# A second, narrower form for pairs of experts that hold few tokens

## The chip, the cores and the metric

The kernel runs on one core of one Trainium2 chip (trn2). The metric is device time in microseconds (us) of one execution. Three runs of the kernel before gave 617.62, 618.52 and 620.73 us; the median is 618.52 us.

## What is computed

One layer of a diffusion backbone over 256 tokens of width 1024, all in float32: modulation, a normalisation, three branches (a convolution, a neighbourhood attention, a recurrence), and then a mixture of 16 experts, which is what the change touches:

```python
    out = jnp.zeros_like(h)
    for e in range(N_EXPERTS):
        he = jax.nn.silu(h @ w1[e]) * (h @ w3[e])
        out = out + gate[..., e:e + 1] * (he @ w2[e])
    return out
```

`h` is 256 x 1024, `w1` and `w3` are 1024 x 512 and `w2` is 512 x 1024 for each expert. `gate` is zero but for the two experts that the router picks for a token, so an expert has to work on its own tokens alone. How many these are depends on the data. With the inputs that the reference draws, the fuller expert of the pairs 0 to 7 (experts 0 and 1, 2 and 3, and so on) holds 55, 42, 15, 14, 49, 72, 29 and 41 tokens.

## The kernel before

The whole program is one function, `tile_kernel`. Its first 370 us compute the branches and are not touched. After the router, the experts are done in eight pairs, `p` = 0 to 7, one after the other. TensorE (PE) executes its instructions in the order in which the code is written; the other engines are ordered by the scheduler of the recording layer.

**The weights.** A pair has 24 tiles of 128 x 1024 floats (512 KB): eight of `w1`, eight of `w3` (`i` = 0, 1) and eight of `w2` (`i` = 2). All 192 are read in the order of `ew_order` (L102): the pairs in turn, and in a pair `w1`, `w3`, `w2`. On chip there is room for 35 of them (`SPAN`, L111) and two more that are placed at the start. `freed(n)` (L1347) tells that n tiles are done with, and `load_experts` (L117) issues the next n loads, the first 31 from GpSimd's queue (POOL), the others from SyncE's (SP). A load waits for the instructions that last read the tile whose place it takes; eight loads at most are under way, since each waits for the one eight before it.

**One pair.** An expert gets 64 columns for its tokens. `open_group` (L1337) gathers the tokens of two pairs (PE product with a one-hot matrix, ACT writes `xg`). `pair_slots` (L1343) transposes the one-hot matrix (`oT`) and gathers the gates (`gsl`). `product` (L1153) multiplies: for each eighth `k` of the 1024 inputs one matmul for each expert `s` of the pair, the expert's 64 token columns as weights in one half of the array, 512 columns of `w1` or `w3` streamed. The two experts' matmuls stand in different halves of the array's columns. `silu` (L1166), `weigh` (L1169), `hidden` (L1173: transposes, and ACT copies to `heT`), `rows` (L1180: the products with `w2`, q = 0, 1 for the two halves of the output, f = 0 to 3 for its four tiles), `split_rows` (L1186: ACT and DVE write the result `ys` in two parts) and `scatter` (L1190: PE puts the rows back to their tokens with `oT`, DVE adds to the output `xl`) end the pair.

**More than 64 tokens.** `extra` (L1204) does 32 further tokens of each expert, in four column groups: the two experts by two halves of the width (`phe`, `pye`). It stands in conditionals on the number of tokens, which every engine reads into a register (`count`, L1308); `further` (L1315) nests them up to 256 tokens. In `second` (L1326) this ladder is one branch of a conditional, and `w3`'s product without extra tokens the other. `expect` (L1311) writes a hint for PE ahead of the branch.

**The order of PE.** In the loop of L1366, pair p's `w3` product is followed by the next group's gather (after odd p), the next pair's slots, `hidden`, `rows`, then two steps of the next pair's `w1` product (`ahead`), the scatter of pair p, and the rest of the next `w1` product. So PE has matmuls of the next pair while ACT and DVE split this pair's rows. Of the 24 tiles of a pair p > 1, `freed(16)` stands behind `second`, and `freed(8)` behind the rows; for p < 2 three times 8.

**Pair 7** has its own form: halves of 256 columns, `last_rows` and `finish` by quarters of the output, and the output's DMAs.

Of the kernel before, what the change touches and what calls it, by code (L numbers as in the profile page):

```python
# [10 lines left out]
F32R = mybir.dt.float32r  # L11
# [39 lines left out]
def tile_kernel(ctx, tc, x_all, cc, vecs, mod_a, mod_b, w_k, w_rx, w_v, w_in, rnn_w, rpb_t, w_br, w_out,  # L51
# [9 lines left out]
    def mm_bank(shape=(128, 512), name="mm"):  # L61
        return psum.tile(list(shape), F32, tag="mm", name=name, bufs=4)
# [1090 lines left out]
    def product(p, i, ph, h=None):  # L1153

        xg, xo = group[p // 2][0], p % 2 * 128
        cols = slice(0, 512) if h is None else slice(256 * h, 256 * h + 256)
        for k in range(KD):
            for s in range(2):
                c = xo + 64 * s
                w, at = quarter(p, i, s, k, h or 0)  # L1160
                at = at if h is not None else slice(at.start, at.start + 512)
                pe.matmul(ph[64 * s:64 * s + 64, cols], xg(k)[:, c:c + 64], w[:, at], start=k == 0 and not h,  # L1162
                          stop=k == KD - 1, skip_group_check=True)
            yield

    def silu(ph, c=slice(0, 512)):  # L1166
        act.activation(sl[:, c], ph[:, c], AF.Silu)  # L1167

# [11 lines left out]
    def rows(p, py, f, q):  # L1180

        for s in range(2):
            pe.matmul(py[q][64 * s:64 * s + 64, :], heT[f // 2][:, f % 2, 64 * s:64 * s + 64],  # L1183
                      ew[p][2][f][s][:, q * 512:q * 512 + 512], start=f == 0, stop=f == 3, skip_group_check=True)

    def split_rows(py, q):  # L1186
        c = slice(q * 512, q * 512 + 512)
# [112 lines left out]
    def run(steps):  # L1300
        for _ in steps:
            pass
# [7 lines left out]

    def expect(p):  # L1311

        tc.mark_branch_hint_location(f"more{p}", hint=counts[p] > 64, engines=(mybir.EngineType.PE,))

    def further(p, n):  # L1315

# [5 lines left out]
    def more(p):  # L1322

        further(p, 64)

    def second(p, ph0, ph):  # L1326

        with tc.If(counts[p] > 64, label=f"more{p}") as c:
            extra(p, 64, product(p, 1, ph))
            further(p, 96)  # L1330
            silu(ph0)
        with c.Else():
            silu(ph0)
            for _ in product(p, 1, ph):
                pass
# [7 lines left out]
    def pair_slots(p):  # L1343
        c = p % 2 * 128
        return slots(p, [x[:, c:c + 128] for x in group[p // 2][1]], 64)

    def freed(n):  # L1347
        room[0] += n
        load_experts()
# [13 lines left out]
            more(0)  # L1363
    oT, gsl = pair_slots(0)
    run(w1)
    for p in range(7):  # L1366
        ph = mm_bank(name="ph1")
        if p > 1:
            second(p, ph0, ph)
            freed(16)  # L1370
        else:

            if p:
                more(p)
            freed(8 if p else 8 - len(brief))
            silu(ph0)
            run(product(p, 1, ph))
            freed(8)
        for q in range(2):
            weigh(gsl, ph, q)  # L1380
        if p % 2:
            run(open_group(p // 2 + 1))
        oT_ = oT
        oT, gsl = pair_slots(p + 1)
        ph0 = mm_bank(name="ph0")
        w1 = product(p + 1, 0, ph0, 0 if p == 6 else None)
        for q in range(2):
            hidden(q)
        py = [ax_bank(name="py0"), ax_bank(name="py1")]
        for q in range(2):  # L1390
            for f in range(4):
                rows(p, py, f, q)
            split_rows(py, q)
        freed(8)

        ahead(w1, 2)
        scatter(lambda i, m: ys[i][:, m * 128:m * 128 + 128], lambda m: oT_)
        count(p + 1)
        ahead(w1, 1)
        expect(p + 1)  # L1400
        run(w1)


    more(7)
# [150 lines left out]
```

## Time and profile before

| what | us |
|---|---|
| median of three runs | 618.52 |
| the profiled execution, its own time | 616.12 |
| its span, first to last instruction | 614.3 |
| outside the span | 1.8 |
| PE busy | 580.2 (94%) |
| DVE, ACT, POOL busy | 349.1, 259.8, 19.4 |
| DMA over the span | 170.65 MB, mean 278 GB/s |

The granted TensorE clock is 0.999 of 2.4 GHz over the span. The page cuts the span in 40 slices: in the last third, where the experts are, PE's digit is 8 or 9 until the last slice and the DMA queues move 400 GB/s and more, but for a slice with 226 GB/s near 540 us. Busy time of PE counts matmuls that overlap in the array once; "x" counts records, and a float32 matmul leaves two of them. A branch is not counted as busy on any engine.

### The profile page before, as it was taken

The numbers are of one execution on the slowest core, as the hardware profiler recorded it, in microseconds if no ns is written. First come the engines' busy times: TensorE is split into PE (matmuls) and PEld (weight loads), VectorE is DVE, ScalarE is ACT, GpSimd is POOL, SyncE is SP. The second block draws the span as 40 slices with busy tenths as digits, with TensorE's granted clock in tenths as the row PEclk, the third lists the DMA queues.
The fourth block names the chain that finished last, engine by engine and source line by source line (L and its number), as shares of the span: only waits on it lengthen the run. The fifth ranks groups of instructions, "written<-read, shape, count | busy, mean of one in ns | idle before, by whom it ended". The sixth has DMA issues, their size and how long they took to land. (4 is left out here: it accounts for less than half of the span.)

```text
span 614.3 us, 10619 instructions
## 1 busy us (share of the span) xinstructions
PE 580.2 (94%) x4127; PEld 408.1 (66%) x4127; DVE 349.1 (57%) x797; ACT 259.8 (42%) x456; POOL 19.4 (3%) x42
## 2 busy tenths in 40 slices
PE   1899999999999899999999988999999999999986
PEld 0789888778788778888899975335445334454454
DVE  4667899999758968988469554121240314132303
ACT  4345446654598765877545624203012111130101
POOL 0000000000000000103112010000000000000000
PEclk9999999999999999999999999999999999999999
DMA  8983874446853463759969776999999999969961
GB/s 256 367 339 114 310 259 154 137 141 193 278 212 103 138 241 103 236 176 356 313 211 379 283 245 226 388 360 406 402 393 407 407 408 409 398 226 409 409 248 68
DMA packets 51825, 170.65 MB, mean 278 GB/s; under 512 B 5664, under 2 KB 10016, under 8 KB 51744
## 3 DMA queue, kind: packets, MB, share of 16 engines
q1 hardware_dynamic: 46704, 151.26, 67.2%
q0 software_dynamic: 5040, 18.35, 8.6%
q8 instruction: 46, 0.75, 0.5%
q14 instruction: 35, 0.29, 0.1%
HBM read 168.54 MB, written 1.05 MB: 276 GB/s over the span
## 5 line engine op out<-in xcount | busy, mean ns | idle before, releaser
L1162 PE MATMUL ph<-ew,xg 128*64 128x512 f32 (+1 forms) x576 | 115.6, 548 | 3.5 <-PEq L1318 2.8
L73 ACT ACTIVATE w<-raw 128x1024 fp32r<-128x1024 f32 x68 | 71.8, 1056 | 65.6 <-PE gps L69 11.6
L74 DVE TENSOR_TENSOR w<-raw,w 128x1024 fp32r<-128x1024 f32 x68 | 82.9, 1219 | 21.5 <-ACT w L73 20.8
L1162 PEld LDWEIGHTS ph<-ew,xg 128*64 128x64 f32 x576 | 41.5, 137 | 66.0 <-issue 58.3
L70 PE MATMUL gps<-h,w 128*128 128x256 f32 x192 | 55.2, 288 | 1.2 <-DVE w L74 1.2
L68 PE MATMUL gps<-h,w 128*128 128x256 f32 x192 | 56.0, 291 | 0.4 <-DVE y L934 0.4
L69 PE MATMUL gps<-h,w 128*128 128x256 f32 x192 | 54.5, 284 | 0.0
L593 DVE SCALAR_TENSOR_TENSOR cacc<-up,vc,cacc 128x243 f32<-128x243 f32 (+14 forms) x120 | 52.1, 472 | 1.4 <-ACT cacc L585 0.7
L1171 DVE SCALAR_TENSOR_TENSOR he<-sl,gsl,ph 128x256 f32<-128x256 f32 x16 | 7.1, 477 | 77.5 <-PE ph L1162 76.2
L1183 PE MATMUL py<-ew,heT 128*64 128x512 f32 x224 | 49.6, 595 | 1.2 <-ACT heT L1178 0.8
L74 DVE TENSOR_TENSOR ys<-py,ys 128x512 fp32r<-128x512 f32 (+1 forms) x18 | 11.4, 633 | 58.0 <-ACT ys L73 58.0
L68 PEld LDWEIGHTS gps<-h,w 128*128 128x128 f32 x192 | 36.6, 191 | 4.2 <-issue 2.6
L70 PEld LDWEIGHTS gps<-h,w 128*128 128x128 f32 x192 | 36.7, 191 | 2.8 <-issue 1.5
L69 PEld LDWEIGHTS gps<-h,w 128*128 128x128 f32 x192 | 36.7, 191 | 0.9 <-issue 0.7
L1183 PEld LDWEIGHTS py<-ew,heT 128*64 128x64 f32 x224 | 15.5, 137 | 30.8 <-issue 26.0
L1201 DVE SCALAR_TENSOR_TENSOR xl<-scp,g,xl 128x256 f32<-128x256 f32 x72 | 29.2, 475 | 7.5 <-PE scp L1197 7.5
L1167 ACT ACTIVATE sl<-ph 128x512 f32<-128x512 f32 (+1 forms) x9 | 5.0, 550 | 63.1 <-PE ph L1162 40.4
L73 ACT ACTIVATE ys<-py 128x512 fp32r<-128x512 f32 (+1 forms) x18 | 9.9, 550 | 50.5 <-PE py L1183 36.6
L114 POOL DMA_DIRECT2D ew<-in_w_exp x31 | 16.6, 537 | 321.1 <-ACT pp L813 248.8
L1119 ACT ACTIVATE xg<-gps,b2m 128x256 f32<-128x256 f32 x32 | 13.4, 471 | 22.7 <-PE gps L1115 21.8
L349 PE MATMUL mps<-ma,cs 128*32 128x256 f32 (+1 forms) x160 | 10.1, 397 | 13.2 <-DMA ma<-in_mod_a 13.1
L1197 PEld LDWEIGHTS scp<-oT,ys 128*128 128x128 f32 x128 | 15.7, 188 | 6.7 <-issue 5.2
(358 smaller groups left out, 1310.0 us busy)
## 6 DMA issues: line engine op xcount, KB each, us to landing
ew<-in_w_exp SPq DMA_DIRECT2D x161, 512.0 KB, 10.2
raw<-in_w_in SPq DMA_DIRECT2D x40, 512.0 KB, 4.4
ew<-in_w_exp POOLq DMA_DIRECT2D x31, 512.0 KB, 7.3
raw<-in_mod_b SPq DMA_DIRECT2D x28, 512.0 KB, 4.1
ma<-in_mod_a SPq DMA_DIRECT2D x12, 512.0 KB, 10.0
raw<-in_w_br SPq DMA_DIRECT2D x12, 512.0 KB, 4.0
raw<-in_w_out SPq DMA_DIRECT2D x8, 512.0 KB, 7.5
ma<-in_mod_a SPq DMA_DIRECT2D x8, 256.0 KB, 6.7
```

The source lines that it names most:

```text
L68: pe.matmul(ps, wh, xh, start=start, stop=False, skip_group_check=True)
L69: pe.matmul(ps, wh, xl_, start=False, stop=False, skip_group_check=True)
L70: return pe.matmul(ps, wl, xh, start=False, stop=stop, skip_group_check=True)
L73: act.activation(hi, src, AF.Copy)
L74: dve.tensor_tensor(lo, src, r32(hi), op=ALU.subtract)
L114: queue.dma_start(t, w_exp[6 * p + 2 * i + s, :, 1024 * q:1024 * q + 1024])
L593: dve.scalar_tensor_tensor(cacc[:, b, i0:i1], up[:, b, i0 + o:i1 + o], half_d[:, b * 31 + j:b * 31 + j + 1], cacc[:, b, i0:i1], op0=ALU.mu ...
L1119: act.activation(place(k0 + j), ps[:, j, :], AF.Identity, bias=b2m[:, k0 + j:k0 + j + 1])
L1162: pe.matmul(ph[64 * s:64 * s + 64, cols], xg(k)[:, c:c + 64], w[:, at], start=k == 0 and not h, stop=k == KD - 1, skip_group_check=True)
L1183: pe.matmul(py[q][64 * s:64 * s + 64, :], heT[f // 2][:, f % 2, 64 * s:64 * s + 64], ew[p][2][f][s][:, q * 512:q * 512 + 512], start=f == ...
L1197: pe.matmul(ps[:, j, :], rows_(i, m), toks(m), start=(j == 0 and i == 0), stop=i == parts - 1, skip_group_check=True)
L1201: dve.scalar_tensor_tensor(xl[:, m, :], ps[:, j, :], g2[:, m:m + 1], xl[:, m, :], op0=ALU.mult, op1=ALU.add)
```

## The change

Pair 0 stays, pair 7 stays, and pairs 1 to 6 get two conditionals in a row: more than 32 tokens takes `wide_pair`, fewer than 33 takes `narrow_pair`. `wide_pair` has the products of before. `narrow_pair` gives each expert 32 columns and splits the width over two column groups, so that four matmuls (two experts by two halves) stand in the array side by side; it moves a copy of `oT` and `gsl` up by 32 partitions with POOL (`oTb`), so that the scatter finds the second half of the output in the other column group.

What crosses from one pair to the next moves with it: the `w1` product of the next pair no longer starts behind the rows, the previous pair's scatter stands in front of the conditional (eight blocks of the output for odd p, four for even p, whose other four stand inside), and the 24 tiles are freed together behind both conditionals. The `py` banks come from the other pool.

```diff
+    def product_small(p, i, ph):
+        xg, xo = group[p // 2][0], p % 2 * 128
+        for k in range(KD):
+            for s in range(2):
+                for h in range(2):
+                    w, at = quarter(p, i, s, k, h)
+                    c = 64 * s + 32 * h
+                    pe.matmul(ph[c:c + 32, :256], xg(k)[:, xo + 64 * s:xo + 64 * s + 32], w[:, at], start=k == 0,
+                              stop=k == KD - 1, skip_group_check=True)
...
+    def rows_small(p, py):
+        for f in range(4):
+            for s in range(2):
+                for q in range(2):
+                    c, x = 64 * s + 32 * q, 64 * s + 32 * (f // 2)
+                    pe.matmul(py[c:c + 32, :], heT[0][:, f % 2, x:x + 32], ew[p][2][f][s][:, q * 512:q * 512 + 512],
+                              start=f == 0, stop=f == 3, skip_group_check=True)
...
-    for p in range(7):
-        ph = mm_bank(name="ph1")
-        if p > 1:
-            second(p, ph0, ph)
-            freed(16)
-        else:
-            if p:
-                more(p)
-            freed(8 if p else 8 - len(brief))
-            silu(ph0)
-            run(product(p, 1, ph))
-            freed(8)
+    def wide_pair(p, oT, oTb, gsl, toks, ms):
+        ph0, ph = mm_bank(name="ph0"), mm_bank(name="ph1")
+        pool.tensor_copy(oTb, oT)
+        w1 = product(p, 0, ph0)
+        ahead(w1, 1)
+        expect(p)
+        run(w1)
+        second(p, ph0, ph)
+        guess(f"narrow{p}", counts[p] < 33)
         for q in range(2):
             weigh(gsl, ph, q)
-        if p % 2:
-            run(open_group(p // 2 + 1))
-        oT_ = oT
-        oT, gsl = pair_slots(p + 1)
-        ph0 = mm_bank(name="ph0")
-        w1 = product(p + 1, 0, ph0, 0 if p == 6 else None)
+        scatter_rows(toks, ms)
         for q in range(2):
             hidden(q)
-        py = [ax_bank(name="py0"), ax_bank(name="py1")]
+        py = [mm_bank(name="py0"), mm_bank(name="py1")]
         for q in range(2):
             for f in range(4):
                 rows(p, py, f, q)
             split_rows(py, q)
-        freed(8)
-        ahead(w1, 2)
-        scatter(lambda i, m: ys[i][:, m * 128:m * 128 + 128], lambda m: oT_)
+    def narrow_pair(p, oT, oTb, gsl, toks, ms):
+        ph0, ph = mm_bank(name="ph0"), mm_bank(name="ph1")
+        product_small(p, 0, ph0)
+        pool.memset(r32(oTb), 0.0)
+        for s in range(2):
+            a, b = slice(64 * s, 64 * s + 32), slice(64 * s + 32, 64 * s + 64)
+            pool.tensor_copy(oTb[b], oT[a])
+            pool.tensor_copy(gsl[b], gsl[a])
+        silu(ph0, slice(0, 256))
+        product_small(p, 1, ph)
+        weigh(gsl, ph, 0)
+        scatter_rows(toks, ms[:2])
+        hidden(0)
+        scatter_rows(toks, ms[2:])
+        py = mm_bank(name="py0")
+        rows_small(p, py)
+        for q in range(2):
+            split_rows([py, py], q)
...
+    for p in range(1, 7):
+        guess(f"wide{p}", counts[p] > 32)
+        if p % 2 == 0:
+            run(open_group(p // 2))
+        if p > 1:
+            oT, gsl = pair_slots(p)
+        oTb = work.tile([128, T], F32R, name="oTb", bufs=2)
+        n = 8 if p % 2 else 4
+        scatter_rows(toks, range(n))
+        with tc.If(counts[p] > 32, label=f"wide{p}"):
+            wide_pair(p, oT, oTb, gsl, toks, range(n, 8))
+        with tc.If(counts[p] < 33, label=f"narrow{p}"):
+            narrow_pair(p, oT, oTb, gsl, toks, range(n, 8))
+        freed(24)
+        toks = oT, oTb
         count(p + 1)
-        ahead(w1, 1)
-        expect(p + 1)
-        run(w1)
+    expect(7)
+    oT, gsl = pair_slots(7)
+    ph0 = mm_bank(name="ph0")
+    w1 = product(7, 0, ph0, 0)
+    ahead(w1, 2)
+    scatter_rows(toks, range(8))
+    run(w1)
```

`guess` is the hint of `expect` with a label of the caller's. Pair 0 stands in front of the loop, written out: `w3`'s product, `count(1)` and the slots of pair 1, `hidden`, `rows`, with `freed` of 6, 8 and 8 tiles as before.

The order of SyncE's loads, first in the program before, from the load that takes the first place left by pair 1's `w1` onward (`ew` with a number is one weight tile, and the names in brackets are the engines whose counters the load waits for: PE, or the earlier loads DMAHW and DMASW):

```order
L114 DMA ew_6579<-in_w_exp 128x1024 [waits DMAHW4_49,DMASW0_49,PE_49]
L114 DMA ew_6581<-in_w_exp 128x1024 [waits DMAHW5_49,DMASW1_49,PE_49]
L114 DMA ew_6600<-in_w_exp 128x1024 [waits DMAHW6_49,DMASW2_49,PE_49]
L114 DMA ew_6602<-in_w_exp 128x1024 [waits DMAHW7_49,PE_49]
L114 DMA ew_6604<-in_w_exp 128x1024 [waits DMAHW0_49,PE_49]
L114 DMA ew_6606<-in_w_exp 128x1024 [waits DMAHW1_49,PE_49]
```

And in the changed program, the last three loads into places of pair 0 and the first four into places of pair 1:

```order
L114 DMA ew_5540<-in_w_exp 128x1024 [waits DMAHW3_49,DMASW7_49,PE_49]
L114 DMA ew_5542<-in_w_exp 128x1024 [waits DMAHW4_49,DMASW0_49,PE_49]
L114 DMA ew_5544<-in_w_exp 128x1024 [waits DMAHW5_49,DMASW1_49,PE_49]
L114 DMA ew_6741<-in_w_exp 128x1024 [waits DMAHW6_49,PE_49]
L114 DMA ew_6743<-in_w_exp 128x1024 [waits DMAHW7_49]
L114 DMA ew_6745<-in_w_exp 128x1024 [waits DMAHW0_49]
L114 DMA ew_6747<-in_w_exp 128x1024 [waits DMAHW1_49]
```

Before, each load waits for PE at its own place in the pair; now the first of the 24 waits, and the count it waits for is reached in the second half of the narrow form's rows (or when that form has been skipped), so it stands for the whole pair, and those behind it wait only for earlier loads.

The order of PE behind the rows of pair 0, in the program before (`py` the rows, `ph` the `w1` product of pair 1, `scp` the scatter):

```order
L1183 MATMUL py_5496<-ew,heT 64x512 x8
L1162 MATMUL ph_5486<-ew,xg 64x512 x4
L1197 MATMUL scp<-oT,ys 128x256 x16
L1309 TENSOR_LOAD cnt
L1162 MATMUL ph_5486<-ew,xg 64x512 x2
L1313 REGISTER_ALU
L1541 BRANCH_PREFETCH_HINT
L1162 MATMUL ph_5486<-ew,xg 64x512 x10
```

and in the changed program, from the rows of pair 0 to the start of pair 1's `w1` product:

```order
L1195 MATMUL py_5509<-ew,heT 64x512 x8
L1337 REGISTER_ALU
L1618 BRANCH_PREFETCH_HINT
L1218 MATMUL scp<-oT,ys 128x256 x16
L1465 COMPARE_AND_BRANCH
L1162 MATMUL ph_5579<-ew,xg 64x512 x2
```

The four matmuls of the next pair that stood between the rows and their scatter are behind the branch now.

PE in pair 2 of the changed program, from the end of the wide form to the end of the narrow one:

```order
L1195 MATMUL py_7939<-ew,heT 64x512 x8
L1465 UNCONDITIONAL_BRANCH x2
L1467 COMPARE_AND_BRANCH
L1175 MATMUL ph_7961<-ew,xg 32x256 x32
L1175 MATMUL ph_7962<-ew,xg 32x256 x32
L1218 MATMUL scp<-oTb,ys 128x256 x4
L1189 MATMUL hp<-ident,he 128x128 x2
L1218 MATMUL scp<-oTb,ys 128x256 x4
L1204 MATMUL py_8052<-ew,heT 32x512 x16
```

The narrow form stands behind the whole wide form with its ladder of `extra`, so a narrow pair jumps over that, and a wide pair jumps over the narrow form.

## Rows read from the trace of the kernel before

**Rows 1.** The page, part 1, and its DMA issues from POOL.
```profile
PE 580.2 (94%) x4127; PEld 408.1 (66%) x4127; DVE 349.1 (57%) x797; ACT 259.8 (42%) x456; POOL 19.4 (3%) x42
...
ew<-in_w_exp POOLq DMA_DIRECT2D x31, 512.0 KB, 7.3
```

**Rows 2.** Windows: length, PE, PEld, DVE, ACT, POOL busy, clock, DMA share, GB/s.
```profile
404.00:410.00 6.00, 5.96 (x30) 2.08 (x28) 2.50 (x7) 0.00 (x0) 0.00 (x0) 1.00 1.03 409
...
460.00:500.00 40.00, 39.58 (x210) 17.37 (x207) 6.90 (x18) 6.57 (x15) 0.00 (x0) 1.00 1.03 407
...
536.00:547.00 11.00, 10.15 (x75) 7.18 (x72) 4.79 (x11) 4.24 (x10) 0.00 (x0) 1.00 0.51 163
```

**Rows 3.** PE's timeline, end of pair 2 to pair 3's rows: start, length, last waits.
```profile
448.33 7.09 PE L1183 MATMUL py<-ew,heT 128*64 128x512 f32 x32
455.24 1.89 PE L1162 MATMUL ph<-ew,xg 128*64 128x512 f32 x8
457.06 2.15 PE L1197 MATMUL scp<-oT,ys 128*128 128x256 f32 x16
459.14 12.24 PE L1162 MATMUL ph<-ew,xg 128*64 128x512 f32 x56
471.31 4.07 PE L1115 MATMUL gps<-oh,hT 128*128 128x256 f32 x32
475.21 0.38 PE L1141 MATMUL ohp<-ident,oh 128*128 128x128 f32 x2
475.43 0.51 PE L1146 MATMUL pg<-gate,oh 128*128 128x2 f32 x4
```

**Rows 4.** The chain of waits that ended last: start, length.
```profile
587.91 7.13 PE ph L1162 x64
...
606.72 1.90 PE py L1419 x16
```

**Rows 5.** SyncE's weight loads, issued 350 to 410 us, 410 to 441, 535 to 600.
```profile
L114 SPq DMA_DIRECT2D ew<-in_w_exp x28: 327/373/940, 358.2 to 403.0; - x28
...
L114 SPq DMA_DIRECT2D ew<-in_w_exp x25: 327/328/1090, 410.1 to 440.7; - x25
...
L114 SPq DMA_DIRECT2D ew<-in_w_exp x37: 327/328/924, 542.0 to 584.3; - x37
...
DMA to landing us min/median/max: 5.4/10.2/11.9
```

**Rows 6.** PE's timeline, the extra tokens of pair 5: `phe` and `pye` in four column groups.
```profile
517.59 2.13 PE L1220 MATMUL gpe<-hT,ohe 128*128 128x512 f32 x8
...
522.17 7.11 PE L1241 MATMUL phe<-ew,heT 128*32 128x256 f32 x128
...
532.46 3.64 PE L1258 MATMUL pye<-ew,heT 128*32 128x512 f32 x32
...
542.40 4.03 PE L1115 MATMUL gps<-oh,hT 128*128 128x256 f32 x32 [0.85 <-PEq L1318]
```

**Rows 7.** PE's timeline, pairs 0, 4 and 7.
```profile
393.76 7.09 PE L1183 MATMUL py<-ew,heT 128*64 128x512 f32 x32
...
508.39 1.89 PE L1162 MATMUL ph<-ew,xg 128*64 128x512 f32 x8
...
587.91 7.13 PE L1162 MATMUL ph<-ew,xg 128*64 128x256 f32 x64 [2.61 <-PEq L1318]
...
606.65 1.95 PE L1419 MATMUL py<-ew,heT 128*64 128x256 f32 x16
```

**Rows 8.** Groups by form, 380 to 614 us, DVE and ACT: mean ns.
```profile
L74 DVE TENSOR_TENSOR ys<-py,ys 128x512 fp32r<-128x512 f32 x14 | 9.7, 692 | 51.3 <-ACT ys L73 51.3
L1171 DVE SCALAR_TENSOR_TENSOR he<-sl,gsl,ph 128x256 f32<-128x256 f32 x16 | 7.1, 477 | 77.5 <-PE ph L1162 76.2 <-ACT sl L1167 1.3
...
L73 ACT ACTIVATE ys<-py 128x512 fp32r<-128x512 f32 x14 | 8.4, 597 | 43.7 <-PE py L1183 36.6 <-issue 7.1
L1178 ACT ACTIVATE heT<-hp 128x256 f32<-128x256 f32 x16 | 5.9, 388 | 6.2 <-PE hp L1177 6.0
```

**Rows 9.** Branch instructions by source line, PE's: duration ns min/median/max.
```profile
L1318 PEldq COMPARE_BRANCH  x4: 3341/3572/4750, 375.9 to 583.0; - x4
...
L1328 PEldq COMPARE_BRANCH  x6: 89/3688/4074, 435.4 to 559.6; - x6
```

**Rows 10.** The branch of pair 2's `second` on PE.
```profile
L1328 PEldq COMPARE_BRANCH  x1: 3524/3524/3524, 435.4 to 435.4; - x1
```

More of the change, by code (lines that the diff above doesn't have):

```diff
@@ L1311, in expect, with guess @@
     def expect(p):
-        tc.mark_branch_hint_location(f"more{p}", hint=counts[p] > 64, engines=(mybir.EngineType.PE,))
+        guess(f"more{p}", counts[p] > 64)
+    def guess(label, cond):
+        tc.mark_branch_hint_location(label, hint=cond, engines=(mybir.EngineType.PE,))
     def further(p, n):
@@ L1365, in tile_kernel, with scatter_rows @@
     run(w1)
-    for p in range(7):
-        ph = mm_bank(name="ph1")
-        if p > 1:
-            second(p, ph0, ph)
-            freed(16)
-        else:
-            if p:
-                more(p)
-            freed(8 if p else 8 - len(brief))
-            silu(ph0)
-            run(product(p, 1, ph))
-            freed(8)
+    def scatter_rows(toks, ms):
+        scatter(lambda i, m: ys[i][:, m * 128:m * 128 + 128], lambda m: toks[m // 4], ms)
+    def wide_pair(p, oT, oTb, gsl, toks, ms):
[7 more added lines that the diff above has]
+        guess(f"narrow{p}", counts[p] < 33)
         for q in range(2):
             weigh(gsl, ph, q)
-        if p % 2:
-            run(open_group(p // 2 + 1))
-        oT_ = oT
-        oT, gsl = pair_slots(p + 1)
-        ph0 = mm_bank(name="ph0")
-        w1 = product(p + 1, 0, ph0, 0 if p == 6 else None)
+        scatter_rows(toks, ms)
         for q in range(2):
             hidden(q)
-        py = [ax_bank(name="py0"), ax_bank(name="py1")]
+        py = [mm_bank(name="py0"), mm_bank(name="py1")]
         for q in range(2):
@@ L1393, in tile_kernel @@
             split_rows(py, q)
-        freed(8)
-        ahead(w1, 2)
-        scatter(lambda i, m: ys[i][:, m * 128:m * 128 + 128], lambda m: oT_)
-        count(p + 1)
-        ahead(w1, 1)
-        expect(p + 1)
-        run(w1)
+    def narrow_pair(p, oT, oTb, gsl, toks, ms):
[16 more added lines that the diff above has]
+            split_rows([py, py], q)
+    ph = mm_bank(name="ph1")
+    freed(8 - len(brief))
+    silu(ph0)
+    run(product(0, 1, ph))
+    freed(8)
+    for q in range(2):
+        weigh(gsl, ph, q)
+    count(1)
+    toks = oT, oT
+    oT, gsl = pair_slots(1)
+    for q in range(2):
+        hidden(q)
+    py = [mm_bank(name="py0"), mm_bank(name="py1")]
+    for q in range(2):
+        for f in range(4):
+            rows(0, py, f, q)
+        split_rows(py, q)
+    freed(8)
+    for p in range(1, 7):
[13 more added lines that the diff above has]
+        toks = oT, oTb
+        count(p + 1)
+    expect(7)
[5 more added lines that the diff above has]
+    run(w1)
     more(7)
```

## The prediction

> **What bounds the kernel now.** I read the page first, then the windows of the last third, PE's timeline, the chain of waits, and the weight loads of SyncE. The page gives PE 94% busy [rows 1]; for where a saving lands, the windows count. From 460 to 500 us PE is busy 39.58 of 40 us and the DMA queues move 407 GB/s at a share of 1.03 [rows 2]: two resources are full at once. Only from 536 to 547 us do the queues fall to 163 GB/s, while PE goes on. The chain that ended last is PE's matmuls from 587.91 us on [rows 4]. So PE sets the end today, with DMA close behind, and a change that takes work from PE has to be tried against DMA.
>
> Their needs for one pair: a weight tile is 524,288 bytes, at 409 GB/s [rows 2] 1.28 us, so 24 tiles take 30.8 us. PE needs 7.09 for the rows, 1.89 + 12.24 for the two products, 2.15 for the scatter, 0.95 for the slots, about 0.9 for the transposes [rows 3], which is 25.2, and 4.07 for a gather in every second pair: 27.2 on average. PE is the quicker one. It is the bound only because loads run ahead: 31 tiles from POOL [rows 1] and 28 from SyncE were issued by 403.0 us [rows 5], 59 tiles, nearly two and a half pairs, when pair 0 was just done.
>
> **What the change takes away.** In the narrow form the two products are 128 records of 256 columns in four groups, which is what `phe` is in the trace: 7.11 us [rows 6], against 64 records in 14.1 [rows 3]. Its `w2` products are like `pye`, 3.64 us [rows 6] against 7.09. That is 10.5 us of PE for each narrow pair, and with 15, 14 and 29 tokens these are pairs 2, 3 and 6: 31.5 us in all.
>
> **What it adds and moves.** Three things.
>
> First, cover is lost. Before, the next `w1` product stood between rows and scatter, and the slots or the gather between `weigh` and the rows. Now `weigh` (0.48), the transposes (0.9) and ACT's copy (0.39) [rows 3, 8] lie open, 1.8 us a pair; and in odd pairs the scatter waits for the split (0.60 + 0.69) [rows 8], of which the slots hide 0.95.
>
> Second, jumps. A PE branch that falls through takes 0.09 us, one that jumps far 3.3 to 4.75 [rows 9]. The one at 435.4 us cost nothing [rows 10], since most of a `w1` product was queued in front of it: one pair later, in the same order, the products run through without a gap [rows 3]. A narrow pair jumps over the wide form with only the scatter queued: I take 3.5 us open, bounds 0 (covered) and 4.75.
>
> Third, and this decides, the loads. The 24 tiles of a pair were freed in two or three lots, by PE's progress within the pair; now all stand behind the end of the pair (the order of SyncE's queue). With room for 35, only 11 tiles are then still to come when a pair ends, 14 us of DMA.
>
> **The sum, in program time.**
> 1. *End of pair 1.* Pair 0's rows end at 393.76 + 7.09 = 400.85 [rows 7]. The second half of `ys` is there at 402.2, half a scatter later it is 403.3; two products of 7.09 (32 records) give 417.5, the open 1.8 gives 419.3, the rows 426.4. Only now do 24 places come free; before, the first went at 410.1 [rows 5].
> 2. *A hole.* Loads stop at 403.0, at most eight are under way, 8 x 1.28 = 10.2 us. DMA is dry from 413.3 to 426.4, where it moved 409 GB/s before [rows 2].
> 3. *Restart.* The trace has one: issued at 542.0, the first landed 5.4 us later, and the 37th, issued at 584.3, about 10.2 later at 594.5 [rows 5]. That is 52.5 us for 37 tiles.
> 4. *Pair 4.* Its last tile is the 61st after the restart (59 + 61 = 5 x 24): 52.5 + 24 x 1.28 = 83.2, so 509.6. PE would be ready for it about 65 us after 426.4, at 491: 22.2 for pair 2 (gather 4.07, slots 0.95, half a scatter 1.08, jump 3.5, 7.11, 1.8, 3.64), 19.6 for pair 3 by the same prices, and 23.2 for pair 4 up to its rows. **The 21 us that pairs 2 and 3 save on PE turn into waiting for weights.** The first half of the rows ends with that tile and the second takes 3.55: 0.44 + 3.55 more, 513.6. Before, these rows ended about 508.4 [rows 7].
> 5. *Pair 5*, with 72 tokens: slots 0.95, rest of the split 0.4, scatter 2.15, `w1` 7.09, the block with the extra tokens and its jump 542.40 - 517.59 = 24.8 [rows 6], open 1.8, rows 7.09: 44.3, so 557.9.
> 6. *A second hole.* The 96th tile lands at 509.6 + 35 x 1.28 = 554.4, and the next is issued at 557.9. The same tile went at 542.0 before, since 16 of the 24 places came free ahead of the rows. 37 tiles are left: 557.9 + 52.5 = 610.4, against 594.5.
> 7. *The end.* The last quarter's rows need the last tile. Before, they began at 606.65 and the span ended 7.65 later [rows 7]. So 610.4 + 7.65 = 618.0 of span, and with the 1.8 outside it 619.8, against 616.12 of the profiled execution: 3.7 more.
>
> PE alone would be there at about the same time: from 557.9, pair 6 takes 23.2 (gather, slots, scatter, 3.5 of jump, 7.11, 1.8, 3.64), then pair 7 the 27.0 from its start to 606.65, of which 2.61 is a jump [rows 7], and 2.3 for slots and split that lie open: 608 to 610.5, by whether the earlier hint covers that jump. So pair 6's saving is spent too. POOL's copies have the first product's 3.5 us and the second's to hide in; DVE's and ACT's work shrinks; both at nothing.
>
> The median of the three runs is 2.4 above the profiled execution, so the forecast is 618.52 + 3.7 = **622.2 us**, 0.6% slower.
>
> **Rivals.**
> *The end of a wide pair has to jump, slower still.* The count that frees the 24 places is raised behind the jump over the narrow form (82 to 90 matmuls), and pairs 1, 4 and 5 stand in the sum. Three jumps of 3.57 [rows 9] make 10.7: 632.9. For: every far jump in the trace takes that long, hinted or not. Against: 7.09 us of rows are queued before it, and a branch behind some 5 us of queued matmuls was free [rows 3, 10]. It decides if that branch starts later than 3.6 us before the rows end. Chance 0.20. The Trainium skill ("Runtime: NRT & Kernel Launch", section "Instruction fetch mechanics") says that a taken branch outside the fetched pages makes the engine fetch the target before it can go on; the branch rows agree, and by that rule alone each wide pair pays as well, which is this rival.
>
> *No second hole, no change.* Step 6 misses by 3.5 us only. If pair 5 ends by 554.4, DMA never restarts: the last tile comes 37 x 1.28 = 47.4 later, at 601.8, and PE's own chain sets the end, 554.4 + 52.6 (610.5 less 557.9) + 7.65 = 614.7: 0.4 above now, 618.9, or 616.3 if pair 7's jump is covered. For: each term of steps 1 to 5 is good to a microsecond. Against: nothing in pair 5 got shorter. Chance 0.20.
>
> *The saving arrives, faster.* Were the loads far enough ahead, PE would stay the bound: 31.5 less three jumps (10.5) and six pairs' open 1.8 (10.8) leaves 10, so 608. It needs loads that don't stand behind a pair's end, and the queue's order speaks against that. Chance 0.06.
>
> *No pair takes the narrow form.* Then pair 6 is 7 us longer on PE's chain (10.5 less a jump): 617.5 + 7.65 of span, so 629. The counts come from the inputs, and the trace has just one run through `phe`, which fits the one pair over 64. Chance 0.02.
>
> **The numbers.** The forecast keeps 0.52, with a range of its own from 617 to 627: the restart may cost 5.4 us and then 1.28 a tile (51.5 for 37), each jump 0 to 4.75. What a measurement here can tell from no change is about 0.5%, 3.1 us, that is 615.4 to 621.6. Of the 0.52, 0.34 lies above and 0.18 within; of the second rival 0.15 within and 0.05 below; the first and the last are above, the third below. Faster 0.11, same 0.33, slower 0.56. The range of 8 in 10 runs from 614 to 631: it leaves out the whole saving, the case without narrow pairs, and the upper half of the jumps.
>
> **What would show it.** Right: weight loads stop near 403 and start again near 426; DMA at 400 GB/s and more from 432 to 550; PE waits with DMA as releaser in pairs 3 and 4 but not in pair 1; a second pause near 555; the last loads landing near 610, with the last quarter's rows waiting for them. The narrow products must show about 7.1 us for 128 records. Wrong: no pause near 413, loads into pair 1's places while its products run, PE busy above 95% from 430 to 550 us, or a last landing before 600. An end above 628 with PE idle behind branches at the ends of pairs 1, 4 and 5 would be the jumps.

## The result, and the profile after

| | before | after |
|---|---|---|
| median, runs | 619.62 us, 4 | 634.32 us, 4 |
| lowest to highest | 617.62 to 621.63 | 632.03 to 637.04 |
| profiled execution, its span | 616.12, 614.3 | 632.59, 630.8 |
| mean granted TensorE clock | 0.999 | 0.976 |

The ratio is 1.0242, with a 95% interval from 1.0208 to 1.0275: slower, as forecast, but by 14.7 us (16.5 between the profiled executions) where 3.7 were forecast, and past the range's upper end of 631.

The page of the change, part 1 and the queue of instruction fetches (packets, MB, share of the engines); against [rows 1] PE falls from 94% to 90%:

```profile
PE 569.4 (90%) x4313; PEld 409.7 (65%) x4313; DVE 348.6 (55%) x794; ACT 257.7 (41%) x453; POOL 24.9 (4%) x60
...
q8 instruction: 53, 0.87, 0.6%
```

Its windows (columns as in [rows 2]): a dry DMA from 413 us on, then DMA full but PE with gaps, then pair 5's rows and pair 6's products at a lower granted clock.

```profile
413.00:430.00 17.00, 15.32 (x75) 5.64 (x72) 2.25 (x4) 2.13 (x5) 0.00 (x0) 1.00 0.10 23
...
460.00:500.00 40.00, 32.89 (x258) 16.44 (x258) 3.83 (x9) 5.75 (x14) 1.54 (x5) 0.87 1.03 406
...
557.00:565.50 8.50, 8.38 (x34) 2.45 (x32) 0.69 (x1) 1.26 (x3) 0.00 (x0) 0.86 0.04 11
...
579.00:588.00 9.00, 9.00 (x128) 5.00 (x120) 0.00 (x0) 0.38 (x1) 0.97 (x4) 0.76 1.03 411
```

Where before 460 to 500 us had PE busy for 39.58 of 40 us [rows 2], it is now 32.89. SyncE's weight loads (columns as in [rows 5]) stop twice, from 404.7 to 428.1 and from 548.6 to 565.6 us:

```profile
L114 SPq DMA_DIRECT2D ew<-in_w_exp x8: 327/361/373, 399.9 to 404.7; - x8
...
L114 SPq DMA_DIRECT2D ew<-in_w_exp x14: 327/376/737, 428.1 to 440.1; - x14
...
L114 SPq DMA_DIRECT2D ew<-in_w_exp x8: 327/328/328, 539.7 to 548.6; - x8
...
L114 SPq DMA_DIRECT2D ew<-in_w_exp x37: 327/328/650, 565.6 to 608.8; - x37
```

PE's timeline of the change, which answers to [rows 3, 6, 7] (pair 0's rows; pair 1's; the narrow products of pairs 2 and 3; the last of pair 4's rows; pair 5's `phe`, transposes and rows; pair 6's narrow products; pair 7):

```profile
395.34 7.09 PE L1195 MATMUL py<-ew,heT 128*64 128x512 f32 x32
...
420.86 7.09 PE L1195 MATMUL py<-ew,heT 128*64 128x512 f32 x32
...
436.52 2.69 PE L1175 MATMUL ph<-ew,xg 128*32 128x256 f32 x18 [1.40 <-DVEq L1465]
441.18 6.24 PE L1175 MATMUL ph<-ew,xg 128*32 128x256 f32 x110 [1.97 <-issue]
...
463.02 3.16 PE L1175 MATMUL ph<-ew,xg 128*32 128x256 f32 x25 [6.04 <-DVEq L1465]
...
467.98 7.14 PE L1175 MATMUL ph<-ew,xg 128*32 128x256 f32 x103 [1.80 <-issue]
...
513.24 4.51 PE L1195 MATMUL py<-ew,heT 128*64 128x512 f32 x18 [0.21 <-DMA ew<-in_w_exp]
...
532.98 7.11 PE L1262 MATMUL phe<-ew,heT 128*32 128x256 f32 x128
...
556.11 1.14 PE L1189 MATMUL hp<-ident,he 128*128 128x128 f32 x4 [3.76 <-DVE he L1183]
...
559.71 5.75 PE L1195 MATMUL py<-ew,heT 128*64 128x512 f32 x26
...
578.78 9.35 PE L1175 MATMUL ph<-ew,xg 128*32 128x256 f32 x128 [6.09 <-DVEq L1465]
...
602.84 8.81 PE L1162 MATMUL ph<-ew,xg 128*64 128x256 f32 x64 [2.30 <-PEq L1342]
...
623.29 1.95 PE L1496 MATMUL py<-ew,heT 128*64 128x256 f32 x16
```

The three narrow pairs stand still at their entry, L1465, which is the jump over the wide form. By source line and stretch, the branches of the change show on which engine (DVE's time shows between its branch and the semaphore instruction behind it, 457.4 to 462.9 and 573.1 to 578.7 us):

```profile
L1465 PEldq COMPARE_BRANCH  x1: 1425/1425/1425, 434.0 to 434.0; - x1
...
L1465 PEldq COMPARE_BRANCH  x1: 5781/5781/5781, 456.5 to 456.5; - x1
L1465 DVEq COMPARE_BRANCH  x1: 63/63/63, 457.4 to 457.4; - x1
...
L1465 DVEq EVENT_SEMAPHORE  x1: 21/21/21, 462.9 to 462.9; - x1
...
L1465 DVEq COMPARE_BRANCH  x2: 47/55/63, 566.2 to 573.1; - x2
L1465 PEldq COMPARE_BRANCH  x1: 1313/1313/1313, 571.6 to 571.6; - x1
...
L1465 DVEq EVENT_SEMAPHORE  x1: 21/21/21, 578.7 to 578.7; - x1
...
L1342 PEldq COMPARE_BRANCH  x1: 6071/6071/6071, 549.3 to 549.3; - x1
...
L1183 DVEq EVENT_SEMAPHORE  x1: 2497/2497/2497, 553.0 to 553.0; - x1
...
L1467 PEldq COMPARE_BRANCH  x1: 1994/1994/1994, 513.6 to 513.6; - x1
```

From 394 us to the end PE is busy for 198.47 us (before 209.47) and idle for 38.3 (before 10.8): 27.5 more idle less 11.0 of work is the 16.5. Of the 31.5 us of work that the narrow form saves only 11 shows; the two products of the narrow pairs took 8.9, 10.3 and 9.4 us where 7.11 was taken.

Where an instruction waits for a weight tile, the wait can stand in the record of PE's weight load (PEld) and not in that of its matmul. From 426 to 520 us the weight-load records wait 9.3 us for tiles, most of it in these three groups (total us, times, longest):

```profile
PEld py L1195 <- DMA ew<-in_w_exp: 3.4, 4, 1.1
PEld py L1204 <- DMA ew<-in_w_exp: 3.0, 4, 1.2
PEld ph L1162 <- DMA ew<-in_w_exp: 2.7, 5, 1.1
```

### The profile page after: what moved, and what is told of

Its sections match the earlier page's. It is cut to its first block, busy times and chain, and to the rows that moved or that the text cites. A ratio compares the mean times of both kernels' runs of the same rounds, so it can differ in the third digit from the quotient of the medians.

```text
span 630.8 us, 11086 instructions
## 1 busy us (share of the span) xinstructions
PE 569.4 (90%) x4313; PEld 409.7 (65%) x4313; DVE 348.6 (55%) x794; ACT 257.7 (41%) x453; POOL 24.9 (4%) x60
## 5 line engine op out<-in xcount | busy, mean ns | idle before, releaser
L1162 PE MATMUL ph<-ew,xg 128*64 128x512 f32 (+1 forms) x384 | 75.7, 537 | 2.6 <-PEq L1342 2.3
L1162 PEld LDWEIGHTS ph<-ew,xg 128*64 128x64 f32 x384 | 28.6, 140 | 40.6 <-issue 29.6
L1175 PE MATMUL ph<-ew,xg 128*32 128x256 f32 x384 | 28.6, 452 | 17.3 <-DVEq L1465 13.5
L1179 ACT ACTIVATE sl<-ph 128x256 f32<-128x256 f32 (+1 forms) x9 | 4.3, 478 | 78.5 <-PE ph L1175 39.9
L1175 PEld LDWEIGHTS ph<-ew,xg 128*32 128x32 f32 x384 | 15.5, 128 | 29.5 <-issue 16.2
L1195 PE MATMUL py<-ew,heT 128*64 128x512 f32 x128 | 32.3, 615 | 1.4 <-DMA ew<-in_w_exp 0.7
L1195 PEld LDWEIGHTS py<-ew,heT 128*64 128x64 f32 x128 | 9.4, 141 | 21.9 <-issue 16.5
```

The source lines that it names most:

```text
L1175: pe.matmul(ph[c:c + 32, :256], xg(k)[:, xo + 64 * s:xo + 64 * s + 32], w[:, at], start=k == 0, stop=k == KD - 1, skip_group_check=True)
```

## Experiments

All times are medians; ratios are to the kernel before, run on the same chip with them. To compare traces, the ends of stages are counted from the start of pair 0's rows, because what stands ahead of them, the same code in all, took up to 4.8 us longer (393.76 us before, 395.34 in the change). The ends are start plus length in PE's timelines:

| kernel | median, ratio [interval] | pair 1 | pair 4 | pair 5 | last quarter starts |
|---|---|---|---|---|---|
| before | 619.62 | 37.0 | 114.8 | 161.3 | 212.9 |
| forecast for the change | 622.2 | 32.6 | 119.8 | 164.1 | 216.64 |
| the change | 634.32, 1.0242 [1.0208, 1.0275] | 32.6 | 122.4 | 170.1 | 227.95 |
| every pair wide | 637.83, 1.0291 [1.0258, 1.0324] | 32.6 | 122.3 | 170.4 | 231.6 |
| every pair wide, two lots | 635.76, 1.0257 [1.0215, 1.0298] | 32.8 | 119.9 | 170.0 | 228.2 |
| narrow first | 640.09, 1.0317 [1.0275, 1.0359] | 35.2 | 125.7 | 174.7 | 233.0 |
| two lots | 629.39, 1.0155 [1.0126, 1.0185] | 32.8 | 114.5 | 167.5 | 223.9 |
| two lots, narrow first | 623.52, 1.0059 [1.0038, 1.0081] | 35.3 | 115.5 | 164.5 | 216.2 |
| short wide form | 627.41, 1.0135 [1.0091, 1.018] | 32.6 | 120.7 | 169.0 | 221.7 |
| two lots, short | 613.45, 0.9912 [0.9882, 0.9943] | 32.8 | 112.8 | 157.3 | 206.9 |

The forecast stood between two theories: the loads in one lot set the end, or the jumps do.

**Every pair wide.** Both conditions changed, in their notes as well, and nothing else; then the same with the loads in two lots (that edit is shown under "Order and lots").

```diff
-        with tc.If(counts[p] > 32, label=f"wide{p}"):
+        with tc.If(counts[p] > 0, label=f"wide{p}"):
...
-        with tc.If(counts[p] < 33, label=f"narrow{p}"):
+        with tc.If(counts[p] < 1, label=f"narrow{p}"):
```

> Every pair takes the wide form; structure, loads and code sizes are those of the change. This gives up the 10.5 us of PE per narrow pair and with it the three entry jumps. If loads set the end: pairs 2 and 3 take longer on PE but end pair 4 at nearly the same time, 633 to 638. If jumps alone set it: 31.5 us given up, 17 us of stalls and 4 us of slow clock got back, 644 or more. If both: pair 4's rows end within 3 us of 517.7, pair 6 gives up 10.5 and gets back 6.1 and 2.2, 633 to 638.

> Every pair wide, with the loads in two lots (16 behind the products, 8 behind the pair). If loads in one lot are what made the change slow even where no pair is narrow: 8 to 14 us under the run with every pair wide, 624 to 630. If there TensorE's own chain sets the end (its lost cover, the gaps between the pairs' conditionals, pair 5's jump), since it waits for weights only 0.6 us in that run: 634 to 640, no difference.

637.83 and 635.76 us, as the loads or both together would have it in the first, as PE's own chain would in the second. Pair 4's rows end at 122.3 with no narrow pair and at 122.4 with two: **what pairs 2 and 3 save is gone by then, all of it**. All three narrow pairs together are worth 3.5 us, and the two intervals overlap. And a kernel in which no pair is narrow, with its loads in one lot or two, is 16 to 18 us slower than before: that is the price of the two conditionals, the lost cover and the lower clock behind the waits. PE's timeline of the run with every pair wide and two lots shows the largest single wait, in pair 5:

```profile
557.57 1.14 PE L1189 MATMUL hp<-ident,he 128*128 128x128 f32 x4 [4.80 <-DVE he L1183]
558.79 9.49 PE L1195 MATMUL py<-ew,heT 128*64 128x512 f32 x32
```

In the run with one lot PE stands still for more than 0.9 us at a wide pair's end once, at pair 6's; PE's timeline there:

```profile
600.41 0.66 PE L1141 MATMUL ohp<-ident,oh 128*128 128x128 f32 x2 [2.66 <-PEq L1467]
```

**Order and lots.** The narrow form ahead of the wide one; or both forms cut behind the products, 16 tiles freed there and 8 at the end, with SyncE in the program's order (the cut and that order always came together); or both. The edit shown is that of the lots.

```diff
-        with tc.If(counts[p] > 32, label=f"wide{p}"):
-            wide_pair(p, oT, oTb, gsl, toks, range(n, 8))
-        with tc.If(counts[p] < 33, label=f"narrow{p}"):
-            narrow_pair(p, oT, oTb, gsl, toks, range(n, 8))
-        freed(24)
+        with tc.If(counts[p] > 32, label=f"wide{p}"):
+            wide_a(p, oT, oTb, ph0, ph)
+        with tc.If(counts[p] < 33, label=f"narrow{p}"):
+            narrow_a(p, oT, oTb, gsl, ph0, ph)
+        freed(16)
+        with tc.If(counts[p] > 32):
+            wide_b(p, gsl, ph, toks, range(n, 8))
+        with tc.If(counts[p] < 33):
+            narrow_b(p, gsl, ph, toks, range(n, 8))
+        freed(8)
```

> The narrow form stands ahead of the wide one, so a narrow pair no longer jumps over the wide form before its first product; that jump then lies behind its last matmuls. Loads are as in the change, 24 behind a pair's end. If loads set the end (the step of the forecast), only what comes after the second pause counts, and the time falls by less than 4 us, 630 to 634. If the exposed jumps set it, all of the 17 us that PE stood idle at the three entries (1.40 + 1.97, 6.04 + 1.80, 6.09) come back, less some 1 to 2 us for each of three wide pairs that now jump over the narrow form: 612 to 619. If both do (loads up to pair 4's rows, PE from there), what pairs 2 and 3 gain is waited for at pair 4's weights, and only pair 6's 6 us and the slow clock behind it come back: 623 to 628.

> Both forms are cut in two conditionals, products and rest; 16 of a pair's loads stand behind the products' two conditionals and 8 behind the pair's end; SyncE keeps the order of the program. The order wide, narrow stays, so the entry jumps stay. If loads set the end, the first pause shrinks from 18 us to some 8 and the second goes, and the time falls by 8 to 15 us: 619 to 626. If the exposed jumps set it, the time is that of the change or, with two more conditionals a pair, up to 5 us more: 633 to 640. If both do, pair 4 comes some 3 us earlier because PE is then free of the weights, but no more: 628 to 634. In the trace the pauses between 413 and 431 us and between 556 and 570 us must shrink.

> Two lots and the narrow form first. If loads alone set the end: as with two lots alone, 619 to 626. If jumps alone: as with the narrow form first alone, 612 to 619. If both, the two gains add up to more than their sum, since neither pairs 2 and 3 nor pair 6 lose what they save: 603 to 614, which would also be faster than before.

Narrow first alone met no theory: 640.09. The jump over the wide form, moved behind the narrow pair's work, holds DVE there, as PE's timeline shows at the slots of pair 7, and the wide pairs now wait at their entry:

```profile
529.26 8.78 PE L1162 MATMUL ph<-ew,xg 128*64 128x512 f32 x32 [2.09 <-DVEq L1465]
...
603.78 0.66 PE L1141 MATMUL ohp<-ident,oh 128*128 128x128 f32 x2 [8.13 <-DVEq L1467]
```

Two lots brought pair 4's end 7.9 us forward (122.4 to 114.5): the first load after the pause goes 24.0 us after pair 0's rows began, not 32.8. The time, 629.39, lies where "both" had put it, though pair 4 gained 7.9 us and not some 3. Pair 5 gave some 5 of it back, since the added conditionals are jumps too: PE's jump over the unused blocks took 6218 ns at 544.4 us, and one of 2527 ns followed at 551.5. PE's timeline of that run:

```profile
554.91 1.14 PE L1189 MATMUL hp<-ident,he 128*128 128x128 f32 x4 [7.47 <-DVE he L1183]
556.13 9.65 PE L1195 MATMUL py<-ew,heT 128*64 128x512 f32 x32
```

With two lots the order's sign turns: narrow first is 5.9 us quicker (623.52), where with one lot it was 5.8 slower; the 603 to 614 of "both" was missed. PE's waits for DVE's jumps sum to 3.2 us there and to 17.6 with one lot. That this is because the jump, now over half of the wide form, starts beside 7 us of product is argued and was not tried by itself.

**The length of what is jumped over.** The blocks beyond 96 tokens are left out of `second` (no pair has so many): in the change, in the change with two lots, in that with the narrow form first, and in the kernel before.

```diff
             extra(p, 64, product(p, 1, ph))
-            further(p, 96)
```

> The change with the wide form cut short: its blocks for tokens beyond 96 are left out (no pair has so many), so the jump over the wide form in narrow pairs and the jump behind the extra block in pair 5 pass over less code; loads and order are the change's. If the length of a jump decides its price (code that isn't there has to be fetched): the stalls of 6.04 + 1.80 and 6.09 us fall to 2 or less each, the 3.76 us before pair 5's transposes to under 1, and since pairs 2 to 4 are held by the loads, the time falls by pair 5's 3, pair 6's 5 and the slow clock behind it: 621 to 626. If any taken jump costs the same, nothing changes: 632 to 637. If the stalls go and the time stays above 630, the loads set the end behind pair 5 too.

> The change (wide form first) with two lots of loads and with the wide form's blocks beyond 96 tokens left out. Alone, the lots gave 4.9 us (634.3 to 629.4) and the shortening 6.9 (to 627.4). If costs add up: 622.5, give or take 1.5. If two bounds lie side by side and each hides the other's gain: 618 or less. If the loads in two lots leave nothing to gain from the shortening: 627 to 630.

> Two lots, narrow form first, and the wide form's blocks beyond 96 tokens left out. If the length decides: pair 5's 4.70 us before its transposes, the 1.57 and 1.65 behind the narrow pairs and the clock of 0.83 from 550 to 560 us go, which is 8 to 9 us of what is left over 620: 613 to 617, faster than before. If any taken jump costs the same: 621 to 625.

> The kernel before with its blocks beyond 96 tokens left out, as a measure of what leaving them out is worth without the change. If the jump over them lies behind queued work there (0.85 us of TensorE's idle time at 542.40): 617 to 621, no difference. If the code's length costs time in the kernel before too: 612 to 616, and then the gain of the version with two lots and the short wide form would be the shortening's alone.

In the kernel before it changes nothing: 619.39, ratio 0.9996 [0.9972, 1.0019]. In the change it gives 6.9 us (627.41, between the two texts' ranges), with two lots 15.9. With the narrow form first it is 615.21, 0.9924 [0.9898, 0.995]. In PE's timeline of the change with the short form, pair 5's and most of pair 6's stalls are gone, while pair 3's 6 us are still there: PE's own jump takes 6257 ns over less code, so its length doesn't set that one, and the load that the product needs lands just behind it. A wait is new: at the end of pair 4, a wide pair, PE's branch took 5798 ns and left 2.67 us open, and the 4.9 us behind it ran at a granted clock of 0.50, which is 1.2 GHz (the branch by source line, and the window, columns as in [rows 2], stand below PE's lines).

```profile
460.05 4.53 PE L1175 MATMUL ph<-ew,xg 128*32 128x256 f32 x54 [6.02 <-DMA ew<-in_w_exp]
...
517.54 0.66 PE L1141 MATMUL ohp<-ident,oh 128*128 128x128 f32 x2 [2.67 <-PEq L1466]
...
555.04 0.89 PE L1189 MATMUL hp<-ident,he 128*128 128x128 f32 x4 [0.79 <-DVE he L1183]
...
571.84 8.80 PE L1175 MATMUL ph<-ew,xg 128*32 128x256 f32 x128 [1.39 <-DVEq L1464]
```

```profile
L1466 PEldq COMPARE_BRANCH  x1: 5798/5798/5798, 510.8 to 510.8; - x1
...
517.50:522.40 4.90, 4.86 (x23) 4.67 (x23) 2.77 (x8) 0.38 (x1) 0.40 (x1) 0.50 1.02 405
```

PE's timeline with two lots as well: the products of pairs 2, 6 and 7 run at full clock.

```profile
436.81 7.11 PE L1175 MATMUL ph<-ew,xg 128*32 128x256 f32 x128 [1.56 <-PEq L1469]
...
560.96 7.11 PE L1175 MATMUL ph<-ew,xg 128*32 128x256 f32 x128 [0.43 <-PEq L1469]
...
583.88 7.13 PE L1162 MATMUL ph<-ew,xg 128*64 128x256 f32 x64 [3.05 <-PEq L1342]
```

Added up, lots (4.9) and length (6.9) would give 622.5; together they gave 613.45, 9 us more. The time is where two bounds side by side would put it, but the ends show that this is the smaller part. Up to pair 4's end the two gains just add up (1.7 and 7.9 us alone, 9.6 together). Pair 5, from there to its own end, takes 47.7 us in the change, 48.2 with the short form, 53.0 with two lots and 44.5 with both: this is where the 9 us are. Each edit alone had brought a jump into the open there that the run with both does not have, the one at pair 4's end (2.67 us and the slow clock) and the longer one in pair 5 (7.47 us). Only behind pair 5 (57.8, 52.8, 56.4 and 49.6 us) does one bound hide the other: with the short form alone the last tile lands at 615.6 us and the last quarter starts at 615.89.

**Notes for DVE.** Every note of the likely branch given to DVE as well as PE, in the change and in two lots with the narrow form first.

```diff
-        tc.mark_branch_hint_location(label, hint=cond, engines=(mybir.EngineType.PE,))
+        tc.mark_branch_hint_location(label, hint=cond, engines=(mybir.EngineType.PE, mybir.EngineType.DVE))
```

> The change with every note of the likely way given to VectorE too, not to TensorE alone. If VectorE's own unannounced jump over the wide form (5.5 us at 457.4 and at 573.1) is what TensorE waited for: the 6.09 us at pair 6 fall to about 1.4 (TensorE's own jump), pair 3's 6.04 stay for TensorE's own 5.78, the skip of VectorE behind pair 5's extra block shrinks too: 624 to 630. If the notes don't reach VectorE's jumps: 632 to 637, with VectorE's jumps still at 5 us and more.

> Two lots, narrow form first, all code kept, and the notes given to VectorE too. If a note spares VectorE the fetch: as with the code left out, 614 to 619. If not: 621 to 625, with VectorE's jump behind pair 5's extra block still the 4.7 us that TensorE waits for.

633.59 (1.0223 [1.0188, 1.0258]) and 623.16 (1.0051 [1.0024, 1.0078]): no gain, though DVE's jump at pair 6 did shrink. PE's timeline of the first:

```profile
576.93 8.63 PE L1175 MATMUL ph<-ew,xg 128*32 128x256 f32 x128 [1.52 <-DVEq L1465]
...
615.08 1.08 PE L1496 MATMUL py<-ew,heT 128*64 128x256 f32 x6 [0.57 <-DMA ew<-in_w_exp]
```

Neither text on the change was right: the wait at pair 6 fell as the first had it, the time stayed as in the second. The 3.0 us gained behind pair 5 (54.8 to the last quarter, not 57.8) were lost ahead of it (173.4, not 170.1). And more was not to be had: the loads restart with pair 5's end, the last is issued at 612.5 us and lands at 622.6, and the last quarter starts at 622.94. Here the end is the forecast's own, set by the loads' second pause. In the run with two lots the second text was right: 623.16, and pair 5's wait still 4.60 us.

**Keeping every case.** With two lots and the narrow form first: the blocks beyond 96 tokens ahead of the first extra block; the same with three lots in pair 1; those blocks as a loop of five over one block; the loop with the wide form first; and the blocks in a conditional of their own behind the first product (wide form first).

```diff
-            extra(p, 64, product(p, 1, ph))
-            further(p, 96)
+            further(p, 96)
+            extra(p, 64, product(p, 1, ph))
```

```diff
-            further(p, 96)
+            with tc.If(counts[p] > 96):
+                dve.tensor_scalar(posr, pos1[:, :, 2 * p:2 * p + 2], -96.0, None, op0=ALU.add)
+                with tc.For_i(0, 5, 1):
+                    extra(p, 0, at=posr)
+                    dve.tensor_scalar(posr, posr, -32.0, None, op0=ALU.add)
```

```diff
             narrow_a(p, oT, oTb, gsl, ph0, ph)
+        further(p, 96)
+        with tc.If(counts[p] > 32):
+            expect(p)
+            second(p, ph0, ph)
         freed(16)
```

> Two lots, narrow form first, all code kept; in the wide form the blocks beyond 96 tokens stand ahead of the block for 65 to 96 instead of behind it, so that pair 5 jumps over them while its first product is queued. If that jump is what opened 4.70 us before pair 5's transposes and brought the clock of 0.83 behind it: 5 to 7 us under two lots with the narrow form first, 616 to 619, level with before or just under it. If the fetch is then late for the block itself: 621 to 626, with TensorE idle at about 521 us instead.

> As the one before, and in pair 1 the products are two conditionals, with the blocks for extra tokens between them, so that its first 8 loads go a product earlier, by 410 us instead of 421. If loads hold pairs 3 and 4 (TensorE waits for single weight tiles from 470 to 510 us there), these come up to 8 us earlier in DMA and the time falls by 2 to 5: 612 to 616. If TensorE's chain holds, the two added jumps cost 1 to 3 us: 618 to 621.

> Two lots, narrow form first, and the blocks beyond 96 tokens as a loop over one block (five times, within a conditional that no pair takes here), so that the wide form is short and no case is left out. If the length of the code jumped over is what counts: as with the blocks left out or a little more, 614 to 618, faster than before. If jumps cost by their presence: 621 to 625, as with all blocks written out.

> The same loop, two lots, wide form first. If the order of the two forms doesn't matter once the wide form is short: within 2 us of the run with the narrow form first. If the narrow pairs' entry jump still lies open: 3 to 6 us above it, 618 to 624.

> Two lots, wide form first; the wide form is cut after its first product, and between the cut the blocks beyond 96 tokens stand in a conditional of their own, so that no case is left out. If far jumps cost only where no work is queued ahead: the narrow pairs jump over them beside 14 us of products, pair 5 beside 7, and the time is that of the run with the blocks left out plus 1 to 4 us for the added conditionals: 614 to 618. If VectorE's jump over them is late for pair 5's extra block or for the products' weighting: 619 to 624.

They took 621.42 (1.0017 [0.9997, 1.0037]), 622.76 (1.0044 [1.002, 1.0068]), 626.28 (1.0097 [1.007, 1.0124]), 623.06 (1.0071 [1.0044, 1.0099]) and 684.80 us (1.1047 [1.1011, 1.1084]). The first took 2 us off and is level with before, as its second text had it: PE now waits 2.31 us ahead of the first extra block. The next three missed. An earlier first lot brought nothing (pair 4 ended at 117.7, not 115.5). The loop made narrow first 2.8 us slower and wide first 6.3 us quicker than the blocks written out (623.06 against 629.39), so the order matters here too; in the latter pair 5's transposes still wait 7.14 us (7.47 with the blocks written out, 0.85 without them). The last missed by over 60 us: PE's two jumps in a row took 6075 and 7303 ns in pair 3, more than the 7 us of product ahead of them, and PE's timeline shows

```profile
506.58 0.58 PE L1189 MATMUL hp<-ident,he 128*128 128x128 f32 x2 [16.47 <-issue]
```

No version that serves more than 96 tokens beat the kernel before; with the blocks left out, 613.45 is 0.9% under it.

## Why the forecast had the sign and not the size

Against the ends in the table the forecast's steps missed by 0.0 (pair 1), 2.6 (pair 4), 6.0 (pair 5) and 11.3 us (last quarter). The span's 12.8 us over the forecast 618.0 are these 11.3 and 1.6 of the unchanged first part, less 0.1 at the end. What failed is the price of jumps: step 5 took 1.8 us for a wait that measured 5.0, and step 7 had PE level with the loads where it came 4.4 us behind them.

*Steps 1 to 4 held, but for the price of the jumps.* Pair 1's end is right to 0.1 us, the pause is there (23 GB/s from 413 to 430 us), and pair 4 came 2.6 us late, most of it because the 61st tile, the last that its first half of the rows waits for, came at 513.24 us, 85.1 after the restart, not 83.2. "The 21 us that pairs 2 and 3 save on PE turn into waiting for weights": the 21 us did vanish, as the run with every pair wide shows. Part of it went into jumps (3.4 and 7.8 us in the first products of pairs 2 and 3, where 3.5 each was taken) and a slower clock behind them. Another part is waiting for weights, as forecast: PE's matmul records have only 1.4 us of it in pairs 2 to 4, but its weight-load records have 9.3, pair 3's rows took 5.9 us instead of 3.64 and pair 4's 10.9 instead of 7.09, and in two lots pair 4 ended 7.9 us earlier.

*Step 5 failed by 3.4 us.* The "open 1.8" between pair 5's products and rows measured 5.0 (552.35 to 557.34 us). DVE's `weigh` waited for a semaphore that PE raises behind its own jump over the unused blocks. That jump, 3341 ns before [rows 9] and hidden but for 0.85 us, with a gather behind it to cover DVE [rows 6], took 6071 ns at 549.3 us with nothing behind it. With the blocks left out the wait fell from 3.76 to 0.79 us. I had carried the whole block over with its jump as 24.8 us and did not name what had covered it. The rows behind it ran 8.1 us instead of 7.09.

*Step 7 failed by 5.3.* The forecast let the loads set the end and put PE level with them. The last tile was issued at 608.8 us and landed at 618.9, 53.3 after the restart where 52.5 was taken; the last quarter's rows began 4.4 later, at 623.29. PE was later: 6.09 us at pair 6's entry where 3.5 was taken, and two stretches of products at 0.76 to 0.79 of the clock, 9.35 instead of 7.11 and 8.81 instead of 7.13. The mechanism that I missed is **DVE's** jump. I had priced the jumps from PE's rows [rows 9, 10] alone and "DVE's and ACT's work shrinks; both at nothing": true of their work, but DVE takes the same branch with no note ahead, and PE's first product waits for it. With a note for DVE that wait fell from 6.09 to 1.52 us; the loads would have let at most 4.4 us of that reach the end.

*The clock was in no term.* Before, it is 0.999 of 2.4 GHz, and PE never idles for more than 2.6 us in the experts. In the change, stretches that follow 2.3 to 6.1 us of PE idle have a mean granted clock of 0.76 to 0.86, between the levels of 1.2 and 2.4 GHz (0.5 and 1.0); from 590 to 593 us it is back at 1.00. Not every gap costs this: 2.61 us ahead of pair 7's products before [rows 7], and 3.05 in the two-lot short run, were followed by 7.13 us of products, the 7 us of the latter at 1.00.

*The rivals.* Jumps at the ends of wide pairs, the slower rival, were not it in the change: those branches started early enough (513.6 us, with the rows running until 517.7) and took 0.9 to 2.0 us, in line with its own condition, and PE stood still for 0.9 us behind each. Its time, 632.9, came close for another reason: the jumps that cost are at the other side, the narrow pairs' entries and pair 5. Nor was it far off as a mechanism. With the short form pair 4's branch started some 4 us before its rows ended, early enough by the condition, and took 5798 ns; with every pair wide pair 6's took 5792. The condition had taken 3.6 us for the jump.

The rule that the prediction took from the Trainium skill ("Runtime: NRT & Kernel Launch", "Instruction fetch mechanics"), that a taken branch to a target that is not at hand has to wait for its fetch, agrees with the trace at pair 3's entry and in pair 5 (5781 and 6071 ns). By that rule alone wide pairs pay at their ends as well, and there the change's trace shows 0.9 us each and not 3.57.

"The saving arrives" needed loads in finer lots and cheap jumps, and got 613.45 when both were supplied.

*The signs.* The two pauses came, which rules out the rival without the second. The narrow products did not show 7.1 us for 128 records, the last quarter's rows did not wait for the last load, and an end above 628 was to mean idle PE at the ends of pairs 1, 4 and 5, which the trace does not have.

What stays open: why pair 3's note, 5.7 us ahead of its branch like pair 2's 5.3, did not help (5781 ns against 1425), why the branch at a wide pair's end took 5.8 us in two runs and 0.9 to 2.0 in the change, how the notes for DVE cost 3 us up to pair 5, and what decides whether a gap costs the clock.

## What to carry to other kernels

A form that saves matmuls in a data-dependent branch has to be priced by what the branch takes away: work that used to stand across the stage's border, the moment at which buffers come free, and one jump on every engine, not on the bound one alone. Look for the instruction that lies behind a jump and raises a semaphore for another engine. When two edits together give more than their sum, ask in which stage the excess lies before you call it two bounds: here either gave 5 to 7 us and both 21, and most of the excess was jumps in one pair.

## What the runs showed of the hardware

The same far jump did not always cost the same. PE's at the narrow pairs' entries took 1425, 5781 and 1313 ns in the change, DVE's at the last two some 5.5 us; PE's over the unused blocks in pair 5 took 6071. The longest, 7303 ns, is in the run with the blocks' own conditional. The kernel before shows 3.3 to 4.75 us on PE [rows 9]. DVE's branch instruction itself reads as 0.06 us; its wait shows only in the instruction behind it. One of the two queues of instruction fetches carried 53 packets in the change, 50 in the two-lot short run, 65 in the run with the blocks' own conditional, 48 in the run with the narrow form first in one lot, at 640.09 us (so the count alone does not tell the time), and before:

```profile
q8 instruction: 46, 0.75, 0.5%
```
